# Wider matmul operands in a hybrid attention and RWKV-7 layer: 128 rows for the key products, 128 columns for the value products and the key norms

## The chip, the cores and the metric

The kernel runs on one core of one Trainium2 chip. The metric is the device time of one launch in microseconds (us). The core has a matmul engine (TensorE, PE in the rows; its weight loads have a track of their own, PEld), three engines for elementwise work (VectorE = DVE, ScalarE = ACT, GpSimd = POOL) and a queue for transfers (SP). A matmul here is two instructions: a weight load that puts the stationary operand into the array, and the product itself, which streams the moving operand past it.

## The reference

One layer over 2048 tokens of width 1024. After an RMS norm, one projection feeds 8 heads of sliding-window attention and 8 heads of RWKV-7 time mixing; both go through one output projection, then a gated MLP with a causal convolution, then a last RMS norm. The parts that the change touches:

```python
# attention: blocks of 128 queries over 256 keys, 2 key/value groups of 4 heads
s = jnp.einsum('bnqkgd,bnskd->bnkgqs', qb, kb) * (HEAD_DIM ** -0.5)
...
o = jnp.einsum('bnkgqs,bnskd->bnqkgd', p / denom, vb)

# time mixing: per head a state S (64 x 64)
kk = kk / jnp.maximum(jnp.linalg.norm(kk, axis=-1, keepdims=True), 1e-12)
...
def step(S, inp):
    r_t, w_t, k_t, v_t, a_t, b_t = inp
    sa = jnp.einsum('bhvk,bhk->bhv', S, a_t)
    S = S * w_t[:, :, None, :] + sa[..., None] * b_t[:, :, None, :] \
        + v_t[..., None] * k_t[:, :, None, :]
    return S, jnp.einsum('bhvk,bhk->bhv', S, r_t)
```

## The kernel before

The first part of the kernel (some 1,220 us, called the mixer here) does the projection, the attention and the time mixing; the second does the rest of the output projection and the MLP, and the change does not touch it.

The mixer cuts the tokens into 4 blocks of 512 (b) and the time-mixing heads into 4 pairs (j). One pair in one block is a unit; there are 16 (names end in b_j or in j alone). The recurrence is done in 8 chunks of 64 tokens per unit. In one pass of the main loop (L1103) the kernel prepares unit n + 2, builds the products of unit n + 1 (function `t_x`), runs the sequential `chain` of unit n together with its attention heads (`t_attn`), and finishes unit n - 1.

- `t_x` needs, in each chunk and for each of the two heads (hh), the products of the keys with the scaled queries. Tile BK holds both heads' keys (rows 0 to 63 and 64 to 127). Tile W has for each head a 128 x 128 piece per chunk, of which only the head's own 64 rows are filled by VectorE at first (`writes`, tile W in the DVE rows); `px` multiplies over these 64 rows (L790), 4 chunks into one bank, 4 calls per unit, 64 in all. VectorE takes the upper half of the result into XB (L791); ScalarE copies the lower half into the other 64 rows of W (L792), where GpSimd masks it (L793). So the other 64 rows are written only behind the products.
- XB goes through DRAM (tiles dL and LL) into a substitution of 31 steps on VectorE (tiles M and Mt), back through dT and TT, and over two sets of 32-row products (ph) into `chain` of the next pass. This is the long way from px to the recurrence.
- `t_attn`: scores (pS), softmax on VectorE and ScalarE (tiles m and P), a transpose (pT), and `pv`, which multiplies the values by the transposed probabilities into tile pO (L1081): the values vth and vtl hold both groups' 64 columns, and 64 of them are the stationary operand. Each product runs as three passes (`mm3`, high and low parts in fp32r). There are 64 calls, 248 passes of each of the three kinds, 744 in all.
- `pss` (L650) sums the squares of a unit's keys by a product with two columns of ones; ScalarE copies the 2 rows out, and they go through DRAM.

The orders of PE, DVE and ACT in the mixer are written out by the main loop: `slot` gives each piece of side work a place in a pass, the projections (pin_q and the like, three passes of 128 x 128 by 512 per slice) fill the places between, and `in_order` ties each instruction of an engine to the one before. GpSimd and SP are tied so in the first pass alone; later the scheduler of the framework places their instructions. The same PE bank pool (`pre`, two banks) serves px, pss and other small products.

Of the kernel before, what the change touches and what calls it, by code (L numbers as in the profile page):

```python
# [12 lines left out]
AF = mybir.ActivationFunctionType  # L13
# [70 lines left out]
def hybrid_trunk_kernel(  # L84
# [9 lines left out]
    def in_order(key, i):  # L94
        if order["on"]:
            last = order.get(key)
            if last is not None:
                tc.add_manual_dep(i.ins, last.name,
                                  mybir.DependencyInfo(mybir.DependencyClass.NoSync, mybir.DependencyReason.DATA),
                                  reason="issue order")  # L100
            order[key] = i.ins

    def mm(**kw):
        in_order("pe", nc.tensor.matmul(**kw))  # L104
# [4 lines left out]
    def act(*args, **kw):  # L109
        in_order("act", nc.scalar.activation(*args, **kw))  # L110
# [17 lines left out]
    def gordered(name):  # L128
        f = getattr(nc.gpsimd, name)

        def go(*args, **kw):
            i = f(*args, **kw)
            if order.get("prologue", True):
                in_order("pool", i)
        return go
# [4 lines left out]
    gmemset = gordered("memset")  # L140
# [28 lines left out]
    def dma(**kw):  # L169
        i = nc.sync.dma_start(**kw)  # L170
        if order.get("prologue", True):
            in_order("sp", i)
# [16 lines left out]
    def mm3(ps, passes, first=True, last=True, **kw):  # L189
        n = len(passes)  # L190
        for i, (lh, ll, rh, rl) in enumerate(passes):
            mm(out=ps, lhsT=lh, rhs=rh, start=first and i == 0, stop=False, **kw)
            mm(out=ps, lhsT=lh, rhs=rl, start=False, stop=False, **kw)
            mm(out=ps, lhsT=ll, rhs=rh, start=False, stop=last and i == n - 1, **kw)


    with ExitStack() as A:
# [17 lines left out]
        def tmp512(name, dt=F32, n=BLK):  # L215
            return tp.tile([P, n], dt, tag="t", name=name, bufs=3)
# [4 lines left out]
        def pre(name):  # L221
            return ps_pre.tile([P, BLK], F32, tag="pre", name=name)
# [8 lines left out]
        for g, cst in zip(cgroups, csts):  # L231
            o = 0
# [48 lines left out]
        onesb = acon.tile([P, P], F32, name="onesb")  # L281
# [7 lines left out]
        vth = acon.tile([P, 5, P], F32R, name="vth")  # L289
        vtl = acon.tile([P, 5, P], F32R, name="vtl")  # L290
# [6 lines left out]
        hs = [slice(0, 64), slice(64, 128)]  # L297
# [111 lines left out]
        def need(key):  # L409
            while any(d[3] == key for d in todo):  # L410
                todo.pop(0)[2]()
# [214 lines left out]
        def v3(ap):  # L626
            return ap.rearrange("p (c t) -> p c t", t=C)

        def t_prep(F, n):
            b, j = divmod(n, NPAIR)  # L630
            u = f"{b}_{j}"
            jc = slice(j, j + 1)
            js = slice(j * P, (j + 1) * P)
            S = U[n] = {}
# [11 lines left out]
            def pss():  # L646
                need(f"k{j}_{b}")
                need(f"k{j}_{b}")
                ps = pre(f"pss_{u}")
                mm(out=ps[0:2, :], lhsT=onesb[:, ::64], rhs=S["kk2"], start=True, stop=True)  # L650
                ssb = tmp512(f"ssb_{u}")[0:2]
                act(ssb, ps[0:2, :], AF.Copy)
                nd = ddpool.tile([2, BLK], F32, tag="nd", name=f"nd_{u}")
                dma(out=nd, in_=ssb)
                S["nq"] = tp.tile([P, 8], F32, tag="nq", name=f"nq_{u}")
                dma(out=S["nq"], in_=nd.rearrange("h (q t) -> (h q) t", t=8))

# [75 lines left out]
            def ew6():  # L733
                kn = S["kn"] = S["n2b"]
                stt(out=kn, in0=S["k"], scalar=nkk[:, jc], in1=S["n2b"], op0=ALU.mult, op1=ALU.mult)

            S["pss"], S["pw"], S["lora"], S["norm"], S["ew"] = pss, pw_, lora, norm, (ew1, ew2, ew3, ew4, ew5, ew6)
            S["done"] = dict(k=k_done, r=r_done, v=v_done)

        def t_x(F, n):  # L740
            b, j = divmod(n, NPAIR)
            u = f"{b}_{j}"
            S = U[n]
            T_ = {}

            def writes(i):
                def go():
                    if i == 0:
                        need(f"v{j}_{b}")
                        S["W"] = pp.tile([P, NCH, 2, P], F32, tag="W", name=f"W_{u}")  # L750
                        S["XB"] = pp.tile([P, NCH, P], F32, tag="XB", name=f"XB_{u}")
                        S["Bt"] = pp.tile([P, NCH, C], F32, tag="Bt", name=f"Bt_{u}")
                        S["IK"] = IKs[n % 2]
                        S["SV"] = pp.tile([P, NCH, 2, C], F32, tag="SV", name=f"SV_{u}")
                        St = state[j]
                        gcopy(out=S["SV"][0:64, 0, 0, :], in_=St[0:64])
                        gcopy(out=S["SV"][64:128, 0, 1, :], in_=St[64:128])
                    W, E = S["W"], S["E"]
                    s = hs[i % 2]
                    if i < 2:  # L760
                        tt(out=W[s, :, i, 0:C], in0=v3(S["kn"])[s], in1=E[s, :, 0:C], op=ALU.mult)
                    else:
                        tt(out=W[s, :, i - 2, C:2 * C], in0=v3(S["r"])[s], in1=E[s, :, 1:C + 1], op=ALU.mult)
                return go
# [18 lines left out]
            def px(q, hh):  # L783
                def go():
                    cs = slice(4 * q, 4 * q + 4)
                    s, o = hs[hh], hs[1 - hh]
                    W, XB = S["W"], S["XB"]
                    ps = pre(f"px_{u}_{q}_{hh}").rearrange("p (c t) -> p c t", c=4)
                    for c in range(4):
                        mm(out=ps[:, c], lhsT=S["BK"][s, 4 * q + c, :], rhs=W[s, 4 * q + c, hh, :], start=True, stop=True)  # L790
                    tt(out=XB[s, cs, :], in0=ps[0:64], in1=cmb[0:64].broadcast_to([64, 4, P]), op=ALU.mult)  # L791
                    act(W[o, cs, hh, :], ps[64:128], AF.Copy)  # L792
                    gsel(out=W[o, cs, hh, :], in_=W[o, cs, hh, :], pattern=[[0, 4], [1, 2], [1, C]],  # L793
                                            compare_op=ALU.is_gt, fill=0.0, base=0, channel_multiplier=-1)
                return go
# [203 lines left out]
        def t_attn(n):  # L999
            b, j = divmod(n, NPAIR)  # L1000
            S = {}
# [68 lines left out]
            def pv(q2, g):  # L1070
                def go():
                    u = f"{b}_{j}_{q2}_{g}"
                    e0 = 1 if (b == 0 and q2 == 0) else 0
                    assert H["vb"] == b
                    need(f"t_{u}")
                    th, tl = S["th", g], S["tl", g]
                    gs = hs[g]
                    pO = ps_at.tile([P, 2, P], F32, tag="at", name=f"pO_{u}")
                    for e in range(2):
                        qb = 2 * q2 + e  # L1080
                        mm3(pO[0:64, e], [(vth[:, qb + kb, gs], vtl[:, qb + kb, gs], th[:, 2 * e + kb], tl[:, 2 * e + kb])  # L1081
                                          for kb in range(e0 if e == 0 else 0, 2)])
                    act(S["o"][gs, q2 * 256:(q2 + 1) * 256], pO[0:64].rearrange("p e q -> p (e q)"), AF.Copy)
                    if q2 == 1:
                        r0 = 64 * (4 * g + j)
                        dma(out=catT[r0:r0 + 64, b * BLK:(b + 1) * BLK], in_=S["o"][gs])
                return go
# [15 lines left out]
        for n in range(-2, NU + 1):  # L1103
# [50 lines left out]
            if PR:  # L1154
# [25 lines left out]
                S = U[pn]  # L1180
# [69 lines left out]
    with ExitStack() as B:  # L1250
# [84 lines left out]
        def o_job(wo, n):  # L1335
            i, e = OJ[n]
            ps = bank(f"po_{i}_{e}")
            chh, cll = cats.pop(n)
            mm3(ps, [(chh[:, k * P:(k + 1) * P], cll[:, k * P:(k + 1) * P], *wo[k]) for k in range(NK)])
            return ps  # L1340
# [83 lines left out]
        for n in range(len(OJ)):  # L1424
            if n + 1 < len(OJ):
                x_load(n + 1)
            ps = o_job(wo, n)
# [340 lines left out]
        for p in ORDER:  # L1768
# [3 lines left out]
            for k in range(NPR):  # L1772
                if p in (1, 2) and k > 0:
                    f = k - 1 if p == 1 else NPR - 1 + k
# [74 lines left out]
```

## Time and profile before

| | us |
|---|---|
| median of 3 runs (lowest, highest) | 2682.79 (2681.02, 2684.7) |
| profiled execution | 2685.55 |
| its span, first to last instruction | 2683.8 |
| PE busy in the span | 2534.4 |
| DVE busy | 1740.1 |
| POOL busy | 1469.0 |
| ACT busy | 1285.3 |

The profiled execution is one more launch. Busy times add the durations of an engine's instructions where they don't overlap. Matmuls are pipelined: a product's duration runs on into the next one's, so what one costs is read from the distance between the starts of two that follow each other. The granted clock (PEclk) is TensorE's clock as a share of 2.4 GHz; 0.50 is 1.2 GHz.

### The profile page before, as it was taken

The numbers are of one execution on the slowest core, as the hardware profiler recorded it, in microseconds if no ns is written. First come the engines' busy times: TensorE is split into PE (matmuls) and PEld (weight loads), VectorE is DVE, ScalarE is ACT, GpSimd is POOL, SyncE is SP. The second block draws the span as 40 slices with busy tenths as digits, with TensorE's granted clock in tenths as the row PEclk, the third lists the DMA queues.
The fourth block names the chain that finished last, engine by engine and source line by source line (L and its number), as shares of the span: only waits on it lengthen the run. The fifth ranks groups of instructions, "written<-read, shape, count | busy, mean of one in ns | idle before, by whom it ended". The sixth has DMA issues, their size and how long they took to land.

```text
span 2683.8 us, 42227 instructions
## 1 busy us (share of the span) xinstructions
PE 2534.4 (94%) x15211; PEld 1988.0 (74%) x15211; DVE 1740.1 (65%) x3232; ACT 1285.3 (48%) x2753; POOL 1469.0 (55%) x1364
## 2 busy tenths in 40 slices
PE   7799999999999989998989999999999999999997
PEld 5566766767667666776768788787888888888886
DVE  6568776777677757644756777867676765453336
ACT  4356655665556555543434434345343343343343
POOL 6334443444444434321637777777666665564598
PEclk9899998999999989899979999999999999999999
DMA  4222222222223222335662444545233326742354
GB/s 126 62 70 74 74 71 74 66 68 76 70 59 96 64 66 74 80 116 182 189 203 86 157 141 144 161 162 192 83 110 102 118 91 233 237 158 102 102 166 172
DMA packets 333108, 313.94 MB, mean 117 GB/s; under 512 B 102576, under 2 KB 254274, under 8 KB 332898
## 3 DMA queue, kind: packets, MB, share of 16 engines
q1 hardware_dynamic: 332290, 310.71, 38.1%
q8 instruction: 119, 1.95, 0.3%
q14 instruction: 91, 0.75, 0.1%
q10 hardware_dynamic: 608, 0.53, 0.1%
HBM read 229.26 MB, written 81.92 MB: 116 GB/s over the span
## 4 chain that ended last, share of the span: by engine, by line
PE 62%; DVE 17%; DMA 7%; ACT 5%; issue 4%; POOL 4%; SPq 0%; POOLq 0%; ACTq 0%; DVEq 0%
PE q_g L104 14%; PE d L104 14%; PE q_u L104 13%; DVE M L124 4%; DVE Mt L124 4%; PE pin_q L104 3%; PE poa L104 3%; DMA LL<-dL 3%; PE px L104 2%; PE po L104 2%; PE pc L104 2%; DVE P L124 2%; PE pin_k L104 1%; PE ph L104 1%; PE pO L104 1%
## 5 line engine op out<-in xcount | busy, mean ns | idle before, releaser
L1262 POOL TENSOR_TENSOR ul_u<-s_u,uh_u 128x512 fp32r<-128x512 f32 x154 | 214.4, 1401 | 138.0 <-ACT uh_u L110 134.8
L1262 POOL TENSOR_TENSOR ul_a<-sa,uh_a 128x512 fp32r<-128x512 f32 x154 | 210.9, 1377 | 139.7 <-ACT uh_a L110 139.7
L1262 POOL TENSOR_TENSOR ul_g<-s_g,uh_g 128x512 fp32r<-128x512 f32 x154 | 220.9, 1442 | 60.9 <-ACT uh_g L110 54.8
L104 PE MATMUL q_g<-h2h,uh_g 128*128 128x512 f32 x616 | 242.6, 394 | 10.0 <-DVE u_g L1486 5.9
L104 PE MATMUL q_g<-h2l,uh_g 128*128 128x512 f32 x616 | 241.7, 392 | 0.0
L104 PE MATMUL q_g<-h2h,ul_g 128*128 128x512 f32 x616 | 241.5, 393 | 0.1
L104 PE MATMUL q_u<-h2h,uh_u 128*128 128x512 f32 x616 | 240.2, 390 | 1.3 <-DVE ct L1486 1.0
L104 PE MATMUL q_u<-h2h,ul_u 128*128 128x512 f32 x616 | 239.9, 389 | 0.9 <-POOL ul_u L1262 0.9
L104 PE MATMUL q_u<-h2l,uh_u 128*128 128x512 f32 x616 | 239.7, 389 | 0.0
L104 PE MATMUL d<-ul_b,uh_a 128*128 128x512 f32 x616 | 232.9, 390 | 1.8 <-DVE ul_b L1483 1.8
L104 PE MATMUL d<-uh_b,ul_a 128*128 128x512 f32 x616 | 229.5, 389 | 0.0
L110 ACT ACTIVATE uh_a<-sa 128x512 fp32r<-128x512 f32 x154 | 97.1, 631 | 229.1 <-PE d L104 122.3
L104 PE MATMUL d<-uh_b,uh_a 128*128 128x512 f32 x616 | 205.9, 389 | 0.0
L110 ACT ACTIVATE uh_u<-s_u 128x512 fp32r<-128x512 f32 x154 | 95.1, 628 | 223.5 <-DVE s_u L1483 113.8
L124 DVE TENSOR_TENSOR Mt<-M,LL 128x60 f32<-128x60 f32 (+24 forms) x496 | 159.2, 321 | 41.7 <-DMA LL<-dL 33.3
L110 ACT ACTIVATE uh_g<-s_g 128x512 fp32r<-128x512 f32 x154 | 95.3, 629 | 186.3 <-PE q_u L104 102.7
L1483 DVE TENSOR_TENSOR ul_b<-wd,uh_b 128x512 fp32r<-128x512 f32 x55 | 68.6, 1249 | 156.1 <-ACT uh_b L110 150.1
L124 DVE SCALAR_TENSOR_TENSOR cc<-g,fcst,cc 128x1024 f32<-128x1024 f32 x88 | 145.4, 1670 | 29.1 <-ACT cc L110 28.4
L124 DVE TENSOR_TENSOR M<-M,Mt 128x60 f32<-128x60 f32 (+24 forms) x496 | 155.7, 314 | 10.8
L104 PEld LDWEIGHTS q_g<-h2h,uh_g 128*128 128x128 f32 x616 | 117.0, 190 | 36.0 <-DVE u_g L1486 7.2
L104 PEld LDWEIGHTS d<-ul_b,uh_a 128*128 128x128 f32 x616 | 115.6, 188 | 27.8 <-DVE ul_b L1483 4.1
L104 PEld LDWEIGHTS q_u<-h2h,uh_u 128*128 128x128 f32 x616 | 115.6, 188 | 27.2 <-DVE ct L1486 1.4
(371 smaller groups left out, 7017.5 us busy)
## 6 DMA issues: line engine op xcount, KB each, us to landing
sa<-actc SPq DMA_DIRECT2D x77, 512.0 KB
s_g<-in_ffn_w_gate_dram SPq DMA_DIRECT2D x44, 512.0 KB
s_u<-in_ffn_w_up_dram SPq DMA_DIRECT2D x44, 512.0 KB
actc<-cc SPq DMA_DIRECT2D x88, 256.0 KB
actc<-sa SPq DMA_DIRECT2D x66, 256.0 KB
wd<-in_ffn_w_down_dram SPq DMA_DIRECT2D x22, 512.0 KB
s_cat<-catT SPq DMA_DIRECT2D x20, 512.0 KB
x<-in_x_dram SPq DMA_DIRECT2D x16, 512.0 KB
```

The costliest lines, as they stand in the source:

```text
L104: in_order("pe", nc.tensor.matmul(**kw))
L110: in_order("act", nc.scalar.activation(*args, **kw))
L124: in_order("dve", f(*args, **kw))
L1262: return nc.gpsimd.tensor_tensor(out=out, in0=in0, in1=in1, op=ALU.subtract)
L1483: return nc.vector.tensor_tensor(out=out, in0=in0, in1=in1, op=ALU.subtract)
```

## The change

Three products get a wider operand, with the same results in the places that are read.

```diff
@@ pss
-                mm(out=ps[0:2, :], lhsT=onesb[:, ::64], rhs=S["kk2"], start=True, stop=True)
-                ssb = tmp512(f"ssb_{u}")[0:2]
-                act(ssb, ps[0:2, :], AF.Copy)
+                mm(out=ps, lhsT=onesb, rhs=S["kk2"], start=True, stop=True)
+                ssb = tmp512(f"ssb_{u}")
+                act(ssb, ps, AF.Copy)
                 nd = ddpool.tile([2, BLK], F32, tag="nd", name=f"nd_{u}")
-                dma(out=nd, in_=ssb)
+                dma(out=nd, in_=ssb[::64])
@@ t_x, writes(0)
+                        for hh in range(2):
+                            gmemset(S["W"][hs[1 - hh], :, hh, :], 0.0)
                         St = state[j]
@@ t_x, px
-                        mm(out=ps[:, c], lhsT=S["BK"][s, 4 * q + c, :], rhs=W[s, 4 * q + c, hh, :], start=True, stop=True)
+                        mm(out=ps[:, c], lhsT=S["BK"][:, 4 * q + c, :], rhs=W[:, 4 * q + c, hh, :], start=True, stop=True)
@@ t_attn, pv
-                        mm3(pO[0:64, e], [(vth[:, qb + kb, gs], vtl[:, qb + kb, gs], th[:, 2 * e + kb], tl[:, 2 * e + kb])
+                        mm3(pO[:, e], [(vth[:, qb + kb], vtl[:, qb + kb], th[:, 2 * e + kb], tl[:, 2 * e + kb])
                                           for kb in range(e0 if e == 0 else 0, 2)])
-                    act(S["o"][gs, q2 * 256:(q2 + 1) * 256], pO[0:64].rearrange("p e q -> p (e q)"), AF.Copy)
+                    act(S["o"][gs, q2 * 256:(q2 + 1) * 256], pO[gs].rearrange("p e q -> p (e q)"), AF.Copy)
```

The key products (px) now run over all 128 rows: the other head's 64 rows of W are zero when they run, because GpSimd fills them with zeros beforehand (two memsets of 64 x 8 x 128 per unit, 32 in all). The value products (pO) take both groups' 128 columns as the stationary operand, and ScalarE reads the 64 rows of its own group. The key norms (pss) multiply by 128 columns of ones and copy 128 rows out, of which the transfer reads two.

The order of PE and DVE is as it was; in ScalarE's queue and SP's a few neighbouring transfers change places (one place and three). On PE, a first px of a unit now also waits for GpSimd. Here is the piece of PE around the first px of block 1's second unit, before:

```order
L104 MATMUL pin_q_1_4531<-hl_1_2664,wh_q_1_4393 128x512
L104 MATMUL pin_q_1_4531<-hh_1_2663,wl_q_1_4394 128x512
L104 MATMUL px_1_0_0_4539<-W_1_4509,BK_1_4032 128x128 [waits DVE_49]
L104 MATMUL px_1_0_0_4539<-W_1_4509,BK_1_4032 128x128 x3
L104 MATMUL pY_0_4548<-SV_0_3670,W_0_3667 64x64 [waits PE_49,Activation_49]
```

and now, with the wait for the pool engine (Pool):

```order
L104 MATMUL pin_q_1_4543<-hl_1_2670,wh_q_1_4403 128x512
L104 MATMUL pin_q_1_4543<-hh_1_2669,wl_q_1_4404 128x512
L104 MATMUL px_1_0_0_4551<-W_1_4519,BK_1_4042 128x128 [waits DVE_49,Pool_49]
L104 MATMUL px_1_0_0_4551<-W_1_4519,BK_1_4042 128x128 x3
L104 MATMUL pY_0_4560<-SV_0_3678,W_0_3675 64x64 [waits PE_49,Activation_49]
```

Nothing moved there; a wait was added. On GpSimd, the same unit before (kTl is the attention's keys, SV the state of the chain, wl_q and wl_k the low parts of projection weights, M the substitution's tile):

```order
L132 COPY SV_1_4512<-state_142 64x64 [waits PE_49]
L132 CAST kTl<-kTl 64x512 [waits DVE_49,Pool_49]
L132 COPY SV_1_4512<-state_142 64x64
L132 TENSOR_TENSOR wl_q_1_4394<-w_q_1_4174,wh_q_1_4393 128x512 [waits Activation_49,Pool_49]
L132 MEMSET M_1_4640 128x256 [waits DMAHW0_49,DVE_49,PE_49]
L132 TENSOR_TENSOR wl_k_1_4528<-w_k_1_4329,wh_k_1_4527 128x512 [waits DMAHW1_49,PE_49,Activation_49]
```

and now:

```order
L132 MEMSET W_1_4519 64x8x128 [waits PE_49,Pool_49]
L132 CAST kTl<-kTl 64x512 [waits DVE_49]
L132 MEMSET W_1_4519 64x8x128
L132 COPY SV_1_4522<-state_142 64x64 x2
L132 TENSOR_TENSOR wl_q_1_4404<-w_q_1_4184,wh_q_1_4403 128x512 [waits Activation_49,Pool_49]
L132 MEMSET M_1_4652 128x256 [waits DMAHW0_49,DVE_49,PE_49]
L132 TENSOR_TENSOR wl_k_1_4540<-w_k_1_4339,wh_k_1_4539 128x512 [waits DMAHW1_49,PE_49,Activation_49]
```

The two memsets stand ahead of the copies of the state, where GpSimd already waited for PE; what followed them follows still.

## Rows read from the trace of the kernel before

**Rows 1.** The page's first line.
```profile
span 2683.8 us, 42227 instructions
```

**Rows 2.** Busy time, mixer: PE, PEld, DVE, ACT, POOL, PEclk, DMA share, GB/s.
```profile
100.00:1220.00 1120.00, 1043.75 (x8695) 774.30 (x8694) 775.74 (x2164) 653.37 (x1724) 467.70 (x541) 0.96 0.29 75
```

**Rows 3.** What PE waited for, 100 to 1220 us: total, times, longest.
```profile
PE pT L107 <- DVE P L124: 21.5, 19, 3.7
PE pc L104 <- ACT Pt L110: 17.4, 18, 2.8
```

**Rows 4.** The chain that ended last, 0 to 1222 us, by line.
```profile
by line: DVE M L124 8.6%; DVE Mt L124 8.6%; PE pin_q L104 6.3%; DMA LL<-dL 5.7%; PE poa L104 5.4%; issue 5.1%; PE px L104 4.6%; PE pc L104 4.0%; DVE P L124 4.0%; PE pin_k L104 3.0%; PE ph L104 2.5%; PE pO L104 2.3%; DVE m L124 1.8%; PE pin_
```

**Rows 5.** Weight loads by shape, mixer: rows*columns, count, busy us, mean ns.
```profile
L104 PEld LDWEIGHTS px<-W,BK 64*128 64x128 f32 x512 | 63.9, 197 | 19.4 <-issue 5.7 <-POOL BK L132 5.0 <-DVE W L124 3.7
L104 PEld LDWEIGHTS pO<-pth,vth 128*64 128x64 f32 x248 | 34.6, 140 | 7.1 <-DVE M L124 1.7 <-DVE ptl L124 1.6 <-DVE m L124 0.2
...
L104 PEld LDWEIGHTS pS<-kTh,q 128*128 128x128 f32 x128 | 24.0, 188 | 5.4 <-issue 0.7 <-PE pin_r L104 0.7 <-PE pT L107 0.2
...
L104 PEld LDWEIGHTS pss<-kk,onesb 128*2 128x2 f32 x32 | 1.4, 83 | 6.2 <-ACT kk L110 3.4 <-issue 2.1
```

**Rows 6.** PE in order of time, one pO call: start, duration.
```profile
573.10 0.39 PE L104 MATMUL pin_r<-hh,wl_r 128*128 128x512 f32 x1
573.33 0.22 PE L104 MATMUL pO<-pth,vth 128*64 128x128 f32 x1
...
573.99 0.22 PE L104 MATMUL pO<-pth,vtl 128*64 128x128 f32 x1
574.14 0.34 PE L104 MATMUL pc<-SV,W 128*64 128x64 f32 x4
```

**Rows 7.** PE in order of time, scores of 128 by 128 in block 0.
```profile
144.88 0.27 PE L104 MATMUL pS<-kTl,q 128*128 128x128 f32 x1
144.99 0.34 PE L104 MATMUL pS<-kTh,q 128*128 128x256 f32 x1
```

**Rows 8.** PE in order of time, two px calls of different units.
```profile
681.20 0.40 PE L104 MATMUL pin_q<-hh,wl_q 128*128 128x512 f32 x1
681.53 1.16 PE L104 MATMUL px<-W,BK 64*128 64x128 f32 x8
682.61 0.34 PE L104 MATMUL pY<-SV,W 128*64 128x64 f32 x4
...
613.78 1.16 PE L104 MATMUL px<-W,BK 64*128 64x128 f32 x8
614.87 0.50 PE L104 MATMUL pin_k<-hh,wh_k 128*128 128x512 f32 x1
```

**Rows 9.** PE in order of time, t_x's pv: f32 products over 128 rows.
```profile
74.13 0.39 PE L104 MATMUL pin_r<-hh,wl_r 128*128 128x512 f32 x1
74.36 1.05 PE L104 MATMUL pv<-cent,v 128*128 128x128 f32 x8
75.17 0.48 PE L104 MATMUL pin_r<-hh,wh_r 128*128 128x512 f32 x1
```

**Rows 10.** GpSimd's memsets of f32, by shape: count, busy us, mean ns.
```profile
L132 POOL MEMSET M<- 128x256 f32 x16 | 5.0, 312 | 19.3 <-PE ph L104 19.3
...
L132 POOL MEMSET TT<- 128x512 f32 x2 | 1.0, 532 | 0.1
```

**Rows 11.** GpSimd in order of time, ahead of the px at 681.53.
```profile
681.91 1.26 POOL L132 TENSOR_TENSOR wl_k<-w_k,wh_k 128x512 fp32r<-128x512 f32 x1 [7.22 <-ACT wh_k L110]
```

**Rows 12.** Two stretches at a lower clock, columns as in rows 2.
```profile
888.00:891.50 3.50, 3.50 (x14) 2.24 (x14) 1.93 (x3) 2.00 (x4) 2.55 (x3) 0.51 0.10 15
...
1103.00:1116.80 13.80, 13.46 (x60) 10.41 (x61) 4.91 (x8) 4.88 (x11) 8.02 (x9) 0.51 0.14 28
```

**Rows 13.** PE in order of time, px ahead of these two stretches.
```profile
887.21 1.32 PE L104 MATMUL px<-W,BK 64*128 64x128 f32 x8
...
1100.37 2.05 PE L104 MATMUL px<-W,BK 64*128 64x128 f32 x16 [0.20 <-DVE W L124]
```

## The prediction

> **What bounds the kernel now.** I read the busy times first, then what PE waits for, then the chain that ended last, then single calls in order of time. The change touches the mixer alone, some 1,220 of 2683.8 us [rows 1]. From 100 to 1220 us PE is busy for 1043.75 of 1120 us [rows 2], so it waits for 76 us, 4.8 per unit. The waits are for others' results: 21.5 us for P from VectorE, 17.4 for Pt from ScalarE [rows 3]. The chain shows what an added microsecond is worth: M and Mt on VectorE take 17.2% of the 1222 us, the transfer of LL 5.7%, px 4.6% and pO 2.3% [rows 4]. So the path runs in turn through PE and through the substitution with its transfers. PE work counts in full where the path is on PE; elsewhere it counts as far as it outgrows the next wait.
>
> **Value products (pO).** This is the largest term. In the call shown, 12 passes start from 573.33 to 573.99 [rows 6]: 11 distances in 0.66 us, 0.060 us each. The moving operand has 128 columns before and after; what grows is the stationary operand, from 64 to 128 columns. A weight load of 64 columns lasts 140 ns on average, one of 128 columns 188 to 197 ns [rows 5], so about 50 ns more. Do these 50 ns show? The nearest rows are scores of block 0, which are what pO becomes: fp32r, 128 stationary and 128 moving columns. There the distance is 144.88 to 144.99, 0.11 us [rows 7]. So each pass goes from 0.060 to 0.11 us; 744 passes (three kinds of 248, [rows 5] shows one) by 0.05 us are 37.2 us of PE time. The lower bound of this edit is 0, if the wider load hides after all; no row shows one that hides behind 128 moving columns.
>
> How much is on the path? A call takes 573.33 to 574.14, 0.81 us [rows 6], and 64 of them 52 us. The chain holds 2.3% of 1222, 28 us [rows 4], a share of 0.54. So 20 of the 37.2 us count at once. The other 17.2 are 1.1 us per unit against 4.8 us of waits; that covers them if the waits stand behind them and the engines waited for are not late themselves. They partly are, since P and Pt come from PE's own scores and chain products: I let a third through, 6 us (bounds 0 and 17). The term is +26 us, from 20 to 37.
>
> **Key products (px).** Streaming 128 rows costs what 64 rows cost: px runs 8 instructions (two per f32 product) from 681.53 to 682.61, 1.08 us, and pv of the same size, over all rows, 0.81 us from 74.36 to 75.17 [rows 8, 9]. What differs lies at the ends. From a projection to px 0.33 us pass (681.20 to 681.53), from one to pv 0.23; and px to a projection takes 1.09 (613.78 to 614.87), pv to one 0.81, of which some 0.10 is the first load that pv's neighbour hid. So a px with full rows may win 0.10 at its start where a full-array product stands ahead, and 0.18 at its end where one follows. Each of the two calls shown has such a neighbour on one side only: 0.10 and 0.18, 0.14 on average. 64 calls give 9 us, with 0 (if the other neighbours decide) and 64 x 0.28 = 18 as bounds. The chain holds 4.6% of 1222, 56 us, of some 64 x 1.08 = 69, a share of 0.81 [rows 4]: the term is -7 us, from 0 to -15.
>
> The Trainium skill (TensorEngine Tiling (Array Packing), Key Properties) says that a change of tiling mode drains the engine. The start of px agrees. By that rule pO, 64 columns wide between full-width products, would also pay at its start, and full width would win some 0.1 us on each side, 64 x 0.2 = 13 us.
>
> The row for pO does not show it at its start: from pin_r at 573.10 to pO at 573.33 pass 0.23 us [rows 6], the same as into pv. I give pO no such gain.
>
> **Key norms (pss).** 32 instructions over 512 columns stay; their weight loads grow from 83 ns [rows 5] towards 190, and at most one per call, 16 x 0.11 = 1.8 us, is not behind a product. The ends may win what px's do, 16 x 0.2 = 3.2 us. ScalarE's copy has the same 512 columns. I take 0, from -3 to +2.
>
> **Memsets.** 1024 elements per row: 256 take 312 ns and 512 take 532 [rows 10], so 0.86 ns an element and 0.97 us each; two per unit, 31 us on GpSimd in all, which is busy for 468 of 1120 us [rows 2]. They stand ahead of the state copies and M's memset, and behind them comes an idle time of 7.22 us that ends with ScalarE's wh_k [rows 11]. In that time 1.94 us disappear; behind them stand wl_q, whose user is a projection in a later slot, and SV. I cost them at nothing. If that cover is gone, the first px of a unit waits, up to 1.94 us x 16 = 31 us.
>
> **The clock.** Two stretches of 3.5 and 13.8 us ran at a granted clock of 0.51, which is the lower level of 1.2 GHz [rows 12]. Before the first PE ran px from 887.21, before the second px from 1100.37 [rows 13], in both cases with VectorE's or ScalarE's results awaited around it. If full rows keep the clock up there, at most half of 17.3 us comes back, 8.6. But pO's new passes are spread over nearly twice the time, and each new fall of 3.5 us costs up to 1.7. I take -4, from -9 to +4.
>
> **Sum.** 26 - 7 + 0 + 0 - 4 = +15 us. The profiled execution took 2685.55 us, so 2700; it stands 2.8 above the median of the runs, 2682.79. Against the median: 2698 us, 0.6% slower. This measurement tells about 0.2%, 5.4 us, from no change.
>
> **The rivals.**
> 1. Everything passes through: the waits don't take up pO's share off the path, because what PE waits for is itself made from PE's scores. Then pO costs 37; with px at -7 and no gain from the clock +30, 2713 us, up to 2722 with px at 0 and new falls of the clock. For it: 17.4 us of waits are for Pt, and ScalarE's Pt starts from PE's own pc. Against it: substitution and transfers, nearly a quarter of the chain, don't depend on pO.
> 2. The gains cancel it: px at -15, the clock at -9, pss at -3, against pO's 20 on the path: -7, 2676 us; with the middle of these, no change. It needs the neighbours of px to be full-array products on both sides; rows 8 show one side each.
> 3. The wider loads cost nothing (the other side): if a 128-column load hides behind 128 moving columns, pO stays at 0.060 us, and -7 and -4 remain: 2672 us; with full gains 2660. It decides as soon as the distance is under 0.08 us (744 x 0.02 x 0.7 = 10 us). Against it stands the 0.11 of [rows 7].
> 4. px waits for the memsets: slower by up to 31 us more than forecast, 2729 us. It decides where W comes free less than 1.94 us before the first px; for it speaks that the memset waits for PE's last read of W, against it the 7.22 us of idle time.
>
> The Trainium skill (TensorE: Matmul & The Clock Gate, Weight-path perf modes) states a rule that gives rival 3: fast weight load is on when the weights are 128 and the type isn't FP32, with a measured gain of about 2 times. The rows speak against it here: fp32r loads of 128 columns (pS) last 188 ns, longer than the 64-column ones at 140 [rows 5].
>
> **How the numbers follow.** Forecast, +6 to +24: 0.53. Rival 1: 0.16. Rival 2: 0.17, of which 0.11 within 0.2% and 0.06 faster. Rival 3: 0.09. Rival 4: 0.05. Slower by over 0.2%: 0.53 + 0.16 + 0.05 = 0.74; within: 0.11; faster: 0.15. The range is 2677 to 2718: it leaves out rival 3, rival 4, and the upper end of rival 1. The forecast alone has 2689 to 2707.
>
> **What would show it.** pO's passes start 0.11 us apart and its weight loads last about 190 ns; if they start 0.06 apart, the sum's first term is gone. From a projection to px 0.23 us, px to a projection 0.9 or less. The sum of PE's busy time in the mixer grows by some 20 us, and its waits shrink by some 10. The chain holds pO with over 45 us instead of 28. GpSimd's memsets near 0.97 us, and no wait of px for POOL. The granted clock of 0.96 in the mixer stays or rises by 0.01. Wrong would be the forecast if px waits for GpSimd, or if the clock falls in many more places.

## The result, and the profile after

The changed kernel takes 2715.91 us (median of 4 runs, 2714.78 to 2721.81) where the kernel before takes 2683.74 (4 runs): a ratio of 1.0111, with a 95% interval of 1.0088 to 1.0135, so some 30 us slower. The forecast had the sign and half of the size.

The page's first line of the changed kernel, then its busy times in the mixer (columns as in rows 2):

```profile
span 2714.2 us, 42294 instructions
```

```profile
100.00:1220.00 1120.00, 1056.45 (x8515) 804.50 (x8516) 770.25 (x2156) 642.65 (x1693) 486.68 (x561) 0.95 0.28 73
```

In the same 1120 us PE works 12.7 us longer than in [rows 2], and the granted clock is 0.95 instead of 0.96: it was to stay or rise. The first product of the second part (po) starts at 1259.94 us, before at 1230.30. So the mixer grew by 29.6 us and the rest by less than 1. The whole mixer up to that product, before and now:

```profile
0.00:1230.30 1230.30, 1128.14 (x9059) 836.67 (x9059) 840.12 (x2308) 702.96 (x1821) 526.08 (x617) 0.96 0.30 78
```

```profile
0.00:1259.94 1259.94, 1166.31 (x9058) 887.68 (x9059) 842.15 (x2308) 703.94 (x1821) 557.93 (x649) 0.95 0.29 76
```

PE is busy for 38.2 us more (1166.31 against 1128.14) and waits for 93.6 us instead of 102.2. By the clock's records in the two traces, 102 us of the mixer ran at 1.2 GHz before and 123 do now; half of these 20 us, 8 to 10, is the slower clock, so 28 to 30 of the 38 are work. The prediction's own prices make 37 - 9 = 28 of work.

Weight loads of the changed kernel, by shape, which answer to [rows 5]:

```profile
L104 PEld LDWEIGHTS px<-W,BK 128*128 128x128 f32 x480 | 59.5, 194 | 7.5 <-issue 3.5 <-ACT W L110 1.2
...
L104 PEld LDWEIGHTS pO<-pth,vth 128*128 128x128 f32 x240 | 49.1, 205 | 5.6 <-DVE ptl L124 1.5 <-issue 0.7 <-DVE Mt L124 0.5
...
L104 PEld LDWEIGHTS pss<-kk,onesb 128*128 128x128 f32 x28 | 4.6, 188 | 1.0
```

PE in order of time, one pO call and one px call, for [rows 6] and [rows 8]:

```profile
588.83 0.39 PE L104 MATMUL pin_r<-hh,wl_r 128*128 128x512 f32 x1
589.06 0.22 PE L104 MATMUL pO<-pth,vth 128*128 128x128 f32 x1
...
590.24 0.27 PE L104 MATMUL pO<-pth,vtl 128*128 128x128 f32 x1
590.44 0.34 PE L104 MATMUL pc<-SV,W 128*64 128x64 f32 x4
...
698.24 0.40 PE L104 MATMUL pin_q<-hh,wl_q 128*128 128x512 f32 x1
698.47 1.05 PE L104 MATMUL px<-W,BK 128*128 128x128 f32 x8
699.46 0.34 PE L104 MATMUL pY<-SV,W 128*64 128x64 f32 x4
```

Twelve passes of pO start in 1.18 us, 0.107 apart instead of 0.060, and the call takes 1.38 us instead of 0.81. px starts 0.23 us behind its neighbour instead of 0.33, and the next product follows after 0.99 instead of 1.08. So both prices at PE were read rightly: pO's +0.05 per pass, px's gain of 0.1 at the start. Rival 3 falls: the load of 128 columns lasts 205 ns, the one of 64 140. By the rule that the Trainium skill states (TensorE: Matmul & The Clock Gate, Weight-path perf modes) the wide load would have been a fast one, if fp32r doesn't count as FP32. The trace shows no faster load. pO starts 0.23 us behind pin_r, wide as narrow: no gain at its start, as the row had said.

What PE waited for, 100 to 1220 us, against [rows 3], and the chain of the mixer, 0 to 1252 us, against [rows 4]:

```profile
PE pT L107 <- DVE P L124: 19.1, 17, 3.7
PE pc L104 <- ACT Pt L110: 15.7, 15, 2.8
```

```profile
by line: DVE M L124 8.5%; DMA LL<-dL 8.3%; DVE Mt L124 8.1%; PE pin_q L104 6.4%; PE pO L104 5.4%; PE poa L104 4.9%; PE pc L104 4.4%; DVE P L124 3.8%; PE px L104 3.5%; issue 3.1%; PE pin_k L104 2.9%; PE pin_r L104 2.7%; PE ph L104 2.5%; DMA 
```

pO stands in the chain with 5.4% of 1252, 68 us, instead of 28 ("over 45" was named). px fell from 4.6% to 3.5%. GpSimd's memsets, by shape:

```profile
L132 POOL MEMSET W<- 64x1024 f32 x28 | 26.5, 947 | 18.9 <-PE pY L104 17.7
```

947 ns each, as priced (0.97), and no px waits for POOL. The signs at single instructions came out, then, and the clock's did not; nor did PE's busy time in the mixer, which was to grow by some 20 us and grew by 38.

To tell work from clock, I multiply each run's time by its mean granted clock: if PE always worked, the product is the time at 2.4 GHz and the remainder is what the 1.2 GHz stretches took. Where PE waits anyway the remainder is too large, so it is an upper bound. Means over the runs of each kernel, against the runs of before on the same chip (standard errors of the differences 1 to 2 us for products, 1.6 to 4 for remainders); the changed kernel, whose own runs of before are few, is set against the 24 runs of the first group. The groups differ among themselves: before takes 2688 and 2689 us in three of them and 2682 in that of f4 and f5. One launch of before that took 4801 us is left out.

| kernel | ratio to before (95%) | product, us more | remainder, us more |
|---|---|---|---|
| the change | 1.0111 (1.0088 to 1.0135) | +19.0 | +10.5 |
| pO alone (e1) | 1.0085 (1.0067 to 1.0104) | +15.6 | +6.2 |
| px and memsets (e2) | 1.0013 (0.9998 to 1.0027) | +6.5 | -3.6 |
| pss alone (e3) | 1.0001 (0.9979 to 1.0023) | -0.3 | +1.0 |
| all but pO (e4) | 1.0013 (0.9996 to 1.0030) | +7.8 | -4.7 |
| memsets alone (e5) | 1.0060 (1.0037 to 1.0084) | +5.0 | +10.6 |
| pO, calls on the chain (e6) | 1.0107 (1.0080 to 1.0134) | +14.7 | +14.1 |
| pO, calls beside it (e7) | 1.0000 (0.9981 to 1.0019) | -0.2 | -0.6 |
| memsets behind the copies (e9) | 1.0064 (1.0043 to 1.0084) | +5.4 | +11.3 |
| before, 4 waits filled (f1) | 1.0017 (0.9998 to 1.0037) | +13.0 | -8.7 |
| before, 18 places filled (f2) | 0.9986 (0.9970 to 1.0002) | +23.2 | -27.7 |
| the change, filled (f3) | 1.0087 (1.0064 to 1.0111) | +41.8 | -18.8 |
| f2 less the late banks (f4) | 0.9975 (0.9955 to 0.9995) | +19.1 | -26.1 |
| f4 and the chain (f5) | 1.0020 (0.9998 to 1.0042) | +32.4 | -29.1 |

Before has a product of 2609.8 and a remainder of 77.8 us in the first group.

### The profile page after: what moved, and what is told of

It is laid out like the page before. It is cut to its first block, busy times and chain, and to the rows that moved or that the text cites. A ratio compares the mean times of both kernels' runs of the same rounds, so it can differ in the third digit from the quotient of the medians.

```text
span 2714.2 us, 42294 instructions
## 1 busy us (share of the span) xinstructions
PE 2571.3 (95%) x15211; PEld 2039.1 (75%) x15211; DVE 1740.3 (64%) x3232; ACT 1286.0 (47%) x2753; POOL 1500.6 (55%) x1396
## 4 chain that ended last, share of the span: by engine, by line
PE 63%; DVE 18%; DMA 8%; POOL 4%; issue 4%; ACT 3%; SPq 0%; POOLq 0%; ACTq 0%; DVEq 0%
PE q_g L104 14%; PE d L104 14%; PE q_u L104 13%; DVE M L124 4%; DMA LL<-dL 4%; DVE Mt L124 4%; PE pin_q L104 3%; PE poa L104 3%; PE pO L104 3%; PE pc L104 2%; DVE P L124 2%; PE po L104 2%; PE px L104 2%; PE pin_k L104 1%; PE pin_r L104 1%
## 5 line engine op out<-in xcount | busy, mean ns | idle before, releaser
L124 DVE TENSOR_TENSOR Mt<-M,LL 128x60 f32<-128x60 f32 (+24 forms) x496 | 153.7, 310 | 47.1 <-DMA LL<-dL 38.7
L124 DVE SCALAR_TENSOR_TENSOR cc<-g,fcst,cc 128x1024 f32<-128x1024 f32 x88 | 145.2, 1667 | 29.1 <-ACT cc L110 28.4
```

The source lines that it names most:

```text
L124: in_order("dve", f(*args, **kw))
```

## The experiments

### The parts of the change, each alone

**e1: the pO edit alone** (the last hunk of the change on the kernel before).

> Only the value products take 128 columns; px, the memsets and pss are as before. Theory A (everything of pO passes through, because PE's waits move along with it): 744 passes by 0.05 us, +37 us (33 to 40), and the sum of PE's waits in the mixer stays within 5 us of before. Theory B (the forecast's share: half of the calls count in full, a third of the others): +26 us (22 to 30). Theory C (a good part of the loss comes from the other edits or from the clock): +15 to +22 here, and the time at the lower clock in the mixer as before, near 102 us.

Measured 1.0085, +23 us (18 to 28). A falls. The time is at the lower side of theory B, the forecast's share (22 to 30), but the interval takes in the upper part of C too, and the work by itself, a product of 15.6 us, is under B's range: 6.2 us of remainder make up the time. Up to the first po:

```profile
0.00:1253.17 1253.17, 1166.55 (x9058) 878.45 (x9059) 841.72 (x2308) 702.45 (x1821) 529.03 (x617) 0.96 0.29 77
```

PE is busy for 38.4 us more than before, about the 37 that were priced, and waits for 86.6 us instead of 102.2: the waits took up 15.5.

**e2: px over 128 rows, with the memsets it needs; e4: the same and pss; e3: pss alone.**

> Only the key products over 128 rows, with the memsets that they need; pO and pss are as before. Theory A: the ends of px win 0.2 us per run in PE's order, 64 calls in 48 to 64 runs, -7 us (-4 to -11). Theory B: the same -7. Theory C (the memsets or the clock cost time): 0 to +10 us, with px waiting for POOL or more time at 1.2 GHz than before's 102 us.

> The change without its pO edit: px over 128 rows with the memsets, pss with 128 columns. Theory A and B: -7 us (-4 to -11), like px alone, since pss is worth nothing. Theory C: 0 to +15 us.

> Only the key norms with 128 columns of ones and 128 rows copied out. Theory A and B: 0 us (-3 to +2). Theory C: +3 to +8 us, through ScalarE's copy or the transfer of two rows with a step of 64.

e2 and e4 take 3.5 us more than before, e3 nothing; none of the three can be told from no change, but 7 us less are outside the intervals of e2 and e4. Theory A's and B's gain isn't there. Up to the first po of e2:

```profile
0.00:1233.94 1233.94, 1118.80 (x9058) 834.76 (x9059) 842.97 (x2308) 702.55 (x1821) 561.11 (x649) 0.96 0.29 78
```

PE is busy for 9.3 us less than before, in part by the clock, and waits for 115.1 us instead of 102.2. What PE waited for in e2, 100 to 1220 us:

```profile
PE pT L107 <- DVE P L124: 23.5, 20, 3.4
...
PE px L104 <- DVE W L124: 5.3, 10, 0.8
PE pO L104 <- DVE ptl L124: 4.6, 6, 3.0
```

px comes earlier and waits longer for W itself, 5.3 us where the trace of before has 1.9, and pO for ptl 4.6 where it had 0.9: the time won at px's ends turns into waits. The gain is also smaller than priced. In order of time px stands in 43 runs, since 21 of them are two calls back to back, and behind a product of the chain (pc, pY) it starts 0.15 us behind that product in both kernels; the 64 pairs of ends of the forecast aren't there.

**e5: the memsets alone**, px on its 64 rows as before.

```diff
                         S["SV"] = pp.tile([P, NCH, 2, C], F32, tag="SV", name=f"SV_{u}")
+                        for hh in range(2):
+                            gmemset(S["W"][hs[1 - hh], :, hh, :], 0.0)
```

> Only the two memsets of the halves of W per unit are added (nothing reads the zeros; px stays on 64 rows). Theory A and B: GpSimd has the time for 30 us more, 0 us (-2 to +2), and no px waits for POOL. Theory C: +3 to +10 us.

Measured 1.0060, +16 us (10 to 23): more than A and B had, and C's upper end or beyond. I had costed them at nothing, since GpSimd has the time and no px waits for it. Both hold, and they cost all the same: 5.0 us of product and 10.6 of remainder. VectorE's writes of W by input, before and then in e5:

```profile
L124 DVE TENSOR_TENSOR W<-n2b,E 64x512 f32<-64x512 f32 x30 | 25.9, 864 | 1.2
```

```profile
L124 DVE TENSOR_TENSOR W<-n2b,E 64x512 f32<-64x512 f32 x30 | 31.3, 1043 | 1.2
```

The same 30 instructions take 5.4 us longer. GpSimd and VectorE in order of time, in the kernel before:

```profile
538.59 1.30 POOL L132 TENSOR_TENSOR hl<-hr,hh 128x512 fp32r<-128x512 f32 x1 [0.53 <-POOL M L132]
...
538.66 1.78 DVE L124 TENSOR_TENSOR W<-n2b,E 64x512 f32<-64x512 f32 x1
540.37 0.68 DVE L124 TENSOR_TENSOR W<-r,E 64x512 f32<-64x512 f32 x1
541.07 0.69 DVE L124 TENSOR_TENSOR W<-n2b,E 64x512 f32<-64x512 f32 x1
```

and the same place in e5:

```profile
551.33 1.95 POOL L132 MEMSET W<- 64x1024 f32 x2
...
558.38 1.72 POOL L132 TENSOR_TENSOR hl<-hr,hh 128x512 fp32r<-128x512 f32 x1
...
556.58 1.78 DVE L124 TENSOR_TENSOR W<-n2b,E 64x512 f32<-64x512 f32 x1
558.29 0.67 DVE L124 TENSOR_TENSOR W<-r,E 64x512 f32<-64x512 f32 x1
559.00 1.65 DVE L124 TENSOR_TENSOR W<-n2b,E 64x512 f32<-64x512 f32 x1
```

Before, GpSimd's last hl runs beside the first W product of n2b (1.78 us) and is done when the second of n2b starts, at 541.07 (0.69). The two memsets push hl back, and now it lies beside that second one too, at 559.00, which takes 1.65 us. The first px of the unit reads W. The Trainium skill (SBUF — State Buffer, SBUF: two separate sides) says that VectorE and GpSimd share one pair of ports as an exclusive lock, and that a VectorE operation with two SBUF inputs contends only with a GpSimd operation that reads SBUF. The trace agrees: it is hl, which reads, beside which W takes 1.65 and not 0.69 us; the W of r at 558.29, which started before hl, keeps its 0.67, and hl takes 1.72 instead of 1.30.

But this is not shown to be the cost. VectorE has an hl of its own, and n2b just ahead of W; before, and then in e5:

```profile
L124 DVE TENSOR_TENSOR hl<-hr,hh 128x512 fp32r<-128x512 f32 x24 | 21.1, 919 | 1.6 <-ACT hh L110 1.5
...
L124 DVE SCALAR_TENSOR_TENSOR n2b<-k,chan,n2b 128x512 f32<-128x512 f32 x15 | 13.9, 928 | 12.9 <-DMA n2b<-nd 12.8
```

```profile
L124 DVE TENSOR_TENSOR hl<-hr,hh 128x512 fp32r<-128x512 f32 x24 | 17.6, 761 | 7.6 <-ACT hh L110 7.5
...
L124 DVE SCALAR_TENSOR_TENSOR n2b<-k,chan,n2b 128x512 f32<-128x512 f32 x15 | 11.0, 735 | 13.6 <-DMA n2b<-nd 13.5
```

They win 3.5 and 2.9 us, so VectorE loses nothing over the three: the place where the two engines meet has moved. The same W of e2, and of the changed kernel:

```profile
L124 DVE TENSOR_TENSOR W<-n2b,E 64x512 f32<-64x512 f32 x30 | 30.2, 1008 | 1.2
```

```profile
L124 DVE TENSOR_TENSOR W<-n2b,E 64x512 f32<-64x512 f32 x30 | 20.8, 695 | 1.2
```

e2 has nearly all of the longer W (30.2 against 25.9) and costs 3.5 us; the changed kernel has a shorter one, and W of both inputs takes 49.6 us there, as before (49.9). So in the change W is not where the memsets cost, and why they cost in e5 stays open.

**e9: the same memsets behind the copies of the state** instead of ahead of them.

```diff
                         gcopy(out=S["SV"][64:128, 0, 1, :], in_=St[64:128])
+                        for hh in range(2):
+                            gmemset(S["W"][hs[1 - hh], :, hh, :], 0.0)
```

> Only the two memsets per unit, as in the run with the memsets alone, but behind the two copies of the state instead of ahead of them. Theory F (the memsets cost because they stand ahead of the copies and what follows, 2 us late): 0 to +5 us against before. Theory G (they cost because anything that shifts GpSimd's work moves PE's waits against the clock): +8 to +16 us, with the product of time and clock within 5 us of before.

1.0064, with the product 5.4 us and the remainder 11.3 us above before: +17 us (12 to 23). Theory F falls: the place ahead of the copies is not it. G has the sign, with time and product just beyond its bounds. Only this one other place was tried; hl stands behind the memsets in both.

### What the chain says of pO

**e6 and e7: the wide pO in one half of the calls each.** PATH holds the 31 calls that stood on the chain of the kernel before; e7 has `not in`.

```diff
+                        full = 4 * n + 2 * q2 + g in PATH
+                        w, o_ = (slice(0, P), gs) if full else (gs, slice(0, 64))
```

> Wide value products only in those 31 of the 64 calls that stood on the chain that ended last before the change (369 of the 744 passes); everything else as before. Theory A: 369 by 0.05 = 18 us, all of it, +18 us (15 to 21). Theory B (the forecast's step: a call on the path counts in full): +18 us too. If the chain says nothing about what an added microsecond is worth: +13 us or less.

> Wide value products only in the 33 calls that stood beside the chain before the change (375 of 744 passes); everything else as before. Theory A: it costs as much as the other half, +19 us (15 to 22). Theory B (the forecast's step: two thirds go into PE's waits): +6 us (3 to 9). Between them, +9 to +15, the waits take up a part.

e7 costs nothing, with 375 wide passes: neither theory went that far. e6 costs +29 us (21 to 36), more than the 18 that both expected, but only 14.7 of it is product, 0.8 of 369 x 0.05 = 18.5; the rest is remainder. The products of the two add to 14.5, e1's is 15.6. What PE did up to the first po in e7, and in e6:

```profile
0.00:1228.10 1228.10, 1144.89 (x9058) 855.91 (x9059) 840.72 (x2308) 703.03 (x1821) 527.12 (x617) 0.96 0.30 78
```

```profile
0.00:1265.38 1265.38, 1162.81 (x9059) 869.42 (x9059) 842.89 (x2308) 703.20 (x1821) 525.77 (x617) 0.94 0.29 76
```

What it waited for in e7, 100 to 1220 us:

```profile
PE pT L107 <- DVE P L124: 19.6, 19, 3.1
PE pc L104 <- ACT Pt L110: 15.4, 16, 2.8
PE pc L104 <- ACT Ut L110: 6.0, 10, 1.1
PE ph L104 <- DVE T L124: 5.8, 2, 5.5
```

In e7 PE is busy for 16.8 us more than before and waits for 83.2 us instead of 102.2; 1.9 and 2.0 of that are at the two waits of [rows 3], 4.3 and 3.0 at those for Ut and T (10.3 and 8.8 before). In e6 it waits for 102.6, as before. The calls beside the chain stand ahead of waits for other engines, which take them up whole; those on it found no wait that took up theirs. So the chain's calls were the right ones to count, and the third that I let through of the others was nothing.

### The clock

In the trace of before low stretches of the clock follow waits of PE. Three of them, and the stretch around them (columns as in rows 2):

```profile
58.60:65.40 6.80, 6.80 (x26) 5.54 (x25) 3.29 (x4) 1.81 (x3) 3.28 (x4) 0.50 0.13 33
82.50:89.30 6.80, 6.80 (x12) 3.36 (x13) 6.28 (x20) 6.16 (x14) 2.06 (x2) 0.50 0.04 10
...
116.60:126.90 10.30, 10.23 (x86) 7.84 (x87) 4.33 (x6) 2.59 (x7) 2.23 (x7) 0.50 0.16 47
50.00:135.00 85.00, 66.21 (x332) 48.90 (x331) 48.16 (x107) 28.37 (x58) 38.34 (x44) 0.82 0.25 68
```

PE had waited 4.6 us up to 58.30, 3.0 up to 82.47 and 5.2 up to 116.67. **f1 to f5** put idle products into such waits. They read the identity and write what the next real product overwrites, so they leave nothing out and add work; the counts are chosen from the waits of before.

```diff
+        def busy(out, k):
+            for _ in range(k):
+                mm(out=out, lhsT=ident, rhs=ident, start=True, stop=True)
...
+                    if n == 0 and q == 0 and hh == 0:
+                        busy(ps[:, 0], 22)
...
+                    busy(pT[:, e0], {0: 5, 2: 4, 3: 8, 16: 7, 19: 12, 35: 12, 47: 7, 48: 17, 50: 4, 51: 8, 54: 11}.get(4 * n + 2 * q2 + g, 0))
```

> The kernel before, with idle products (identity by identity, f32, 128 columns, some 0.2 us each, into the bank that the next real product overwrites) ahead of four places of the first units where PE waited 3 to 5 us: px of unit 0 (22 products), pss of unit 1 (14), the transposes of x tile 5 (24), ph of unit 0 (25). In the trace of before each of these waits is followed by 7 to 10 us at 1.2 GHz, 31 us together. Theory D (falls of the clock follow PE's waits): these 31 us mostly go, half of them in time, -8 to -15 us. Theory E (the clock falls by something else): 0 to +3 us, with the 31 us still there.

> As the run with four places filled, and also ahead of 11 transposes pT (4 to 17 products), ph of units 8 and 12 (8, 9) and the transposes of x tiles 9 and 13 (7 each), where PE waited 0.7 to 3.7 us before. The waits on Pt and Ut in the chain stay unfilled. Theory D: time at 1.2 GHz in the mixer falls from 102 to 40 to 60 us, and the kernel by 15 us (8 to 25) against before. Theory E: +2 to +8 us.

> The changed kernel with the same idle products. Its time is 30 us above before; multiplied by the mean granted clock it is 18.6 us above, so 10 us would be clock. Theory D: the products take back the clock's 10 us and what they win in the kernel before, +19 - 15 = +4 us against before (-4 to +12), and some 19 us above the filled kernel without the change. Theory E: +30 to +36 us against before.

f1, the same stretches:

```profile
58.60:65.40 6.80, 6.29 (x48) 5.33 (x47) 4.37 (x6) 3.14 (x6) 3.74 (x6) 1.00 0.10 21
82.50:89.30 6.80, 5.94 (x24) 4.04 (x25) 6.28 (x17) 4.72 (x11) 3.54 (x3) 1.00 0.26 78
...
116.60:126.90 10.30, 10.30 (x123) 8.87 (x123) 5.91 (x7) 2.55 (x7) 5.31 (x10) 1.00 0.45 116
50.00:135.00 85.00, 75.26 (x505) 62.50 (x504) 48.96 (x106) 28.28 (x58) 38.64 (x44) 0.94 0.25 66
```

At the three places the clock stays at 2.4 GHz: theory D has the cause right there, and E falls. But the kernel isn't faster (1.0017, where D had 8 to 15 us less): the remainder falls by 8.7 us and the product rises by 13.0. f2 takes 27.7 us out of the remainder and adds 23.2 of work; at 4 us less than before (8 less to 1 more) it misses its 15 too. Part of that work lies behind the wait instead of in it; one row of f2:

```profile
97.36 7.10 PE L104 MATMUL pth<-ident 128*128 128x128 f32 x48 [6.07 <-DVE bv L124]
```

The bank of these transposes came late itself, so the idle products waited 6.07 us with the rest and then cost their full time. f3 falls short of its expectation (+4): the filled change stands 23 us above before. The products win no more there than in the kernel before; f3 lies 18.6 us of product and 8.9 of remainder above f2, nearly the 19.0 and 10.5 that the change costs without them.

**f4** leaves out the products ahead of the late banks, **f5** adds 13 or 7 ahead of five waits on Pt, in a widened part of the chain's bank.

```diff
-                pc = ps_ch.tile([P, 3, C], F32, tag="ch", name=f"pc_{u}_{c}")
+                pc = ps_ch.tile([P, 5, C], F32, tag="ch", name=f"pc_{u}_{c}")
...
+                for _ in range({(1, 5): 13, (5, 5): 13, (9, 5): 13, (2, 4): 7, (6, 4): 7}.get((n, c), 0)):
+                    mm(out=pc[:, 3:5].rearrange("p a b -> p (a b)"), lhsT=ident, rhs=ident, start=False, stop=True, skip_group_check=True)
                 for hh, s in enumerate(hs):
                     mm(out=pc[s, 1], lhsT=TT[s, c, :], rhs=Pt[s], start=False, stop=True, skip_group_check=True)
```

> The kernel before with the idle products of the 18-place run, less those ahead of the transposes of x tiles 5, 9 and 13. There the bank itself was what came late, so that those 38 products (some 8 us) ran behind the wait and filled nothing. Theory D: 4 us better come to some 12 us better than before, -12 us (-7 to -16). If what the products win is only chance: -4 us or less.

> The same, and also 13 or 7 idle products ahead of five of the chain's products that wait 1.7 to 2.8 us for Pt (units 1, 5, 9 in chunk 5, units 2 and 6 in chunk 4), in a part of the bank that nothing reads. Theory D: in the trace of before a stretch of 3.4 us at 1.2 GHz follows three of these waits; 3 to 5 us more than the run without them, -16 us against before (-9 to -21). If the wait on Pt lasts longer with products beside ScalarE's read of the bank: -8 us or less.

f4 is faster than before, 0.9975 (0.9955 to 0.9995), 7 us of the 12 hoped for, and the only version here that beats both kernels clear of noise; its interval of 1 to 12 us overlaps D's range and the 4 us or less of chance alike. Its granted clock in the mixer:

```profile
100.00:1220.00 1120.00, 1062.96 (x9007) 799.91 (x9006) 778.62 (x2159) 655.76 (x1728) 469.90 (x543) 0.98 0.29 76
```

f5 misses. Its products wait for Pt like the one that they were to precede:

```profile
234.18 4.01 PE L104 MATMUL pc<-ident 128*128 128x128 f32 x19 [2.83 <-ACT Pt L110]
```

They write into the tile that ScalarE is reading; they came behind the wait and added 13.3 us of product to f4's.

## Why the prediction was wrong

**The step that failed** is the clock's term: "I take -4, from -9 to +4", and +10.5 was measured. The product, which has the work and the waits at full clock, came out at 19.0 us, as forecast (26 - 7), so the whole miss of some 14.5 us lies there. The prediction asked whether full rows of px keep the clock up, and allowed pO new falls up to +4; the runs show pO losing 6.2 us of remainder by itself (e1), and the memsets 10.6 (e5). Where the clock fell in the three stretches of f1 it followed a wait of PE, and stayed up when the wait was filled: what moves the waits can move the clock. The prediction took the clock from px and from how far pO's passes spread, not from the waits.

**The memsets** at nothing failed with it: alone they cost 16 us (10 to 23), 5.0 of product besides the 10.6. The prediction took the cover at GpSimd (idle time) and at px (no wait for POOL), and both hold. What it left out is the rest of GpSimd's work, which comes 2 us late; what of that costs time stays open. No run has the change without its memsets, so in the change itself their 16 us are not shown.

**px**: -7 forecast, and -4 in the clock's term, which rests on its full rows. From e5 to e2, which add full rows to the same memsets, the time falls by 12.7 us, near these 11, but by another way: the remainder falls by 14.2 and the product rises by 1.6. The 0.1 at each end is in the trace, at 43 pairs of ends instead of 64, and waits took it. With the memsets that it needs, the wide px wins nothing. **pss**: 0 forecast, 0 measured.

**pO**: +26 forecast (20 to 37), +23 measured. Here the steps hold better than their sizes: 20 on the path came to 14.7 of product, the 6 beside it to nothing, and 6 of clock came on top. That all 37 us pass through (rival 1, whose 2713 us fits the time) is refuted by e7: the right number by a wrong mechanism.

**Sum.** That the product is 19.0 where 19 was forecast is luck in part: 15.6 for pO, 6.5 for px with its memsets, 0 for pss make 21.8. In remainder the parts (6.2, -3.6, 1.0) make 3.6 of the 10.5. The 7 us between have a standard error of almost 5; with e4 in place of e2 and e3 they are 9, with an error of 3. The change was not timed in one group with its parts, so how much of its loss belongs to no part alone is not firm. e6 has a larger remainder than e1 (14.1 against 6.2, an error of 4 for the difference), though e1 holds all its wide passes and more: the share may hang on where the waits fall, not on how much is added. Which stretches make up the change's 10.5 us stays open; a trace shows the stretches of one execution, and the idle products, which were sized on the waits of before, didn't take them out of the change.

## What to carry to other kernels

Count an added microsecond by whether the instruction stands on the chain that ended last: the calls beside it cost nothing here, to within 5 us, and those on it 0.8 of their work, with as much again in the clock. For work added to an idle engine, that nobody waits for it doesn't make it free: time it alone. And a small shift can cost more through the granted clock than through any instruction: multiply time by mean clock for both kernels before looking for a cause in the engines.

## What the runs showed of the hardware

- A VectorE product of two SBUF inputs, 64 x 512, took 0.69 us alone and 1.65 to 1.78 beside a GpSimd hl that had started before it (e5).
- The clock's remainder in the kernel before is 78 us of 2688, up to 2.9% of the time. Idle products in PE's waits took 26 us of it away (f4), at 19 us of work.
- A weight load of 128 columns in fp32r took 205 ns here, one of 64 columns 140; products of 128 moving columns started 0.107 us apart behind the wide loads and 0.060 behind the narrow ones.
